# Three column tiles side by side at the head of a recurrent decoder step, with its x loads put in another order

## The chip, the cores and the metric

The kernel runs on one core of a Trainium2 chip. The metric is the device time of one execution in microseconds (us). The kernel before takes 847.57 us, the median of three runs (846.61 to 848.86).

## What is computed

One layer of a hybrid decoder step for a prompt of 256 positions and eight single decode positions, 264 columns in all. A combined projection of x (2048 wide) feeds two branches, an mLSTM and a gated linear attention, whose outputs are gated, projected and normalised:

```python
p = x @ w_in                                   # 2048 -> 12,312 columns
(qk_pre, a_v, a_i, a_f, a_o, a_z, b_q, b_k, b_v, b_g, b_z, g_a, g_b) = _split_cols(p)
conv = causal depthwise conv (width 4) of qk_pre + conv_b
qk = jax.nn.silu(conv)
h, C_new, n_new, m_new = _mlstm(q, k, v, itil, logf, C, n, m)
o, S_new = _gla(gq, gk, gv, loga, S)
merged = jax.nn.sigmoid(g_a) * (ya @ w_pa) + jax.nn.sigmoid(g_b) * (yb @ w_pb)
out = _layernorm(ALPHA * x + merged @ w_out, ln_g, ln_b)
```

## The kernel before

The work is a list of units (line 61), each one tile of 128 output columns: 16 for the convolved q and k, one small one for the gates, then the other projections. A unit has 16 tiles of the contraction, in four chunks of four (`KC`, lines 45 and 46); a chunk of a unit's weights is a piece (line 162), 256 KB. Below, u1c2 is unit 1, chunk 2. x lies in four chunks as well, 528 KB each.

Every fp32 operand is split into a high half (ACT rounds it to fp32r, lines 204 and 211) and a low half (DVE subtracts, lines 206 and 212). `parts` (line 214) then issues three matmuls for each contraction tile: high weights by high x (line 225), high by low (226), low by high (230), 48 for a unit, all into one accumulator of the pool `ps_m`, which has three (line 97). `parts` is a generator: it yields ahead of each chunk, so a caller can interleave units.

Raw weights arrive through `load_raw` (line 167) in tiles of two pieces; there are four such tiles (`RAW_BUFS`). `cast_piece` (line 187) splits the next piece; there are nine buffers for split pieces (`CAST_BUFS`). Its instructions carry a high priority (line 203). The order on PE is that of the source (line 40, `MANUAL`); ACT, DVE and SP get theirs from a planner, by priority and readiness. All loads go through SP's queue.

At the head (lines 1085 to 1099) x is loaded and split chunk by chunk, and units 0 and 1 are worked on side by side: chunk 0 of both, chunk 1 of both, and so on. The first eight pieces are put in that order by line 163. After this the units come one by one (line 1102); units 0 and 1 are only evacuated there. `e_qk` (line 255) evacuates a q or k unit: ACT reads the accumulator (line 261), DVE reads it three times (line 263, the shifted taps), ACT once more (line 266), each of them ahead of the buffer's next use; a sigmoid and a product follow.

Of the kernel before, what the change touches and what calls it, by code (L numbers as in the profile page):

```python
# [23 lines left out]
T = L + NB  # L24
# [20 lines left out]
KC = 4  # L45
NC = KT // KC
KR = 8
RAW_BUFS = 4
CAST_BUFS = 9
LA = CAST_BUFS - NC  # L50
RA = (RAW_BUFS - 1) * KR // KC

COL = {}
# [32 lines left out]
def body(ctx, tc, xT, wbig, wsmall, par, cmask, lmask, sel, rowc, gate, wgu, cT, sT, nst, cst, lnr,  # L86
         y, yd, pC, pn, pm, pconv, pS, sC, sn, sm, sS):
    nc = tc.nc
    V, A, G, PE = nc.vector, nc.scalar, nc.gpsimd, nc.tensor
# [11 lines left out]
    def t4(shape, name, dt=F32):  # L101
        return b4.tile(shape, dt, tag="b4", name=name)
# [21 lines left out]
    def side_ps():  # L124
        return ps_s.tile([128, 512], F32, tag="sd", name="sd")
# [14 lines left out]
    ones = const.tile([128, 128], F32, name="ones")  # L140
# [10 lines left out]
    x_hi = [const.tile([128, 4, T], F32R, name=f"xh{i}") for i in range(4)]  # L151
    x_lo = [const.tile([128, 4, T], F32R, name=f"xl{i}") for i in range(4)]

    def f(ap):
        return ap.bitcast(F32)

    pieces = []
    idx = 0
    for n, (kind, j) in enumerate(UN):
        bi = None if kind == "small" else idx  # L160
        idx += kind != "small"
        pieces += [(n, c, bi) for c in range(NC)]
    pieces[0:2 * NC] = [pieces[u * NC + c] for c in range(NC) for u in range(2)]
    raws, his, los = {}, {}, {}
    nxt = {"dma": 0, "cast": 0}

    def load_raw():
        i = nxt["dma"]
        if i >= len(pieces):
            return  # L170
        r = wraw_p.tile([128, KR, 128], F32, tag="raw", name="raw")
        per = KR // KC
        runs = []
        for q in range(per):
            n, c, bi = pieces[i + q]
            w = 128 if bi is not None else SMALL
            raws[i + q] = r[:, q * KC:q * KC + KC, 0:w]
            if runs and runs[-1][0] == n and runs[-1][2] == c * KC:
                runs[-1][2] += KC
            else:  # L180
                runs.append([n, c * KC, c * KC + KC, q * KC, bi, w])
        for n, k0, k1, o, bi, w in runs:
            src = wbig[bi] if bi is not None else wsmall
            nc.sync.dma_start(out=r[:, o:o + k1 - k0, 0:w], in_=src[:, k0:k1, :])
        nxt["dma"] += per

    def cast_piece():
        i = nxt["cast"]
        while nxt["dma"] <= i:
            load_raw()  # L190
        n, c, bi = pieces[i]
        w = 128 if bi is not None else SMALL
        r = raws.pop(i)
        if bi is None:
            hl = whi_p.tile([128, KC, 128], F32R, tag="hi", name="hl")
            A.copy(out=hl[:, :, 0:w], in_=r)
            V.tensor_tensor(out=hl[:, :, w:2 * w], in0=r, in1=f(hl[:, :, 0:w]), op=ALU.subtract)
            his[n, c], los[n, c] = hl[:, :, 0:2 * w], None
            nxt["cast"] += 1
            return  # L200
        h = whi_p.tile([128, KC, 128], F32R, tag="hi", name="hi")[:, :, 0:w]
        lo = wlo_p.tile([128, KC, 128], F32R, tag="lo", name="lo")[:, :, 0:w]
        with tc.high_priority(offset=PRIO):
            A.copy(out=h, in_=r)  # L204
            E = G if POOL_LO[0] <= n < POOL_LO[1] and c in POOL_C else V
            E.tensor_tensor(out=lo, in0=r, in1=f(h), op=ALU.subtract)  # L206
        his[n, c], los[n, c] = h, lo
        nxt["cast"] += 1

    def split(hi, lo, src):  # L210
        A.copy(out=hi, in_=src)
        V.tensor_tensor(out=lo, in0=src, in1=f(hi), op=ALU.subtract)

    def parts(n, k0, k1, rhs, base=0):

        small = UN[n][0] == "small"
        m = 2 * SMALL if small else 128
        ps = ps_m.tile([128, 512], F32, tag="mm", name="mm")
        out = ps[0:m, 0:T]
        for k in range(k0, k1):  # L220
            if k % KC == 0:
                yield ps[:, 0:T]
            wh = his[n, k // KC][:, k % KC, :]
            rh, rl = rhs(k - base)
            PE.matmul(out, lhsT=wh, rhs=rh, start=(k == k0), stop=False)  # L225
            PE.matmul(out, lhsT=wh, rhs=rl, start=False, stop=small and k == k1 - 1)  # L226
            if small:
                continue
            wl = los[n, k // KC][:, k % KC, :]
            PE.matmul(out, lhsT=wl, rhs=rh, start=False, stop=(k == k1 - 1))  # L230

    def group(*a, **kw):
        for ps in parts(*a, **kw):
            pass
        return ps
# [595 lines left out]
    def e_pab(pa, pb, j):  # L831
        g = gtiles[j // 2]
        i = 2 * (j % 2)
        ga, gb = g[:, i, :], g[:, i + 1, :]
        V.tensor_tensor(out=ga, in0=ga, in1=pa, op=ALU.mult)
        V.tensor_tensor(out=gb, in0=gb, in1=pb, op=ALU.mult)
        V.tensor_tensor(out=ga, in0=ga, in1=gb, op=ALU.add)
        split(mh.t(j), ml.t(j), ga)
# [50 lines left out]
    def ln_shift(j):  # L889

        xt = ln["x", j]
        V.scalar_tensor_tensor(out=xt, in0=xt, scalar=ALPHA, in1=ln["c"], op0=ALU.mult, op1=ALU.subtract)
# [187 lines left out]
    with tc.manual_schedule(engines=MANUAL):  # L1080
        V.memset(ones, 1.0)
        V.memset(inv256, 1.0 / 256.0)
        V.memset(eps_c, EPS)
        V.memset(one_c, 1.0)
        first = [parts(u, 0, 16, x_rhs) for u in range(2)]
        head = {}
        for i in range(4):
            xr = t4([128, 4, T], "xr")
            nc.sync.dma_start(out=xr, in_=xT[:, 4 * i:4 * i + 4, :])
            if 4 * i % KC == 0:  # L1090
                for _ in range(2 * KC // KR):
                    load_raw()
            split(x_hi[i], x_lo[i], xr)
            for u in range(2) if (4 * i + 4) % KC == 0 else ():
                cast_piece()
                head[u] = next(first[u])
        for u in range(2):
            for _ in first[u]:
                pass
        nc.sync.dma_start(out=par_sb, in_=par)  # L1100
        nc.sync.dma_start(out=cst_sb, in_=cst)
        for n, (kind, j) in enumerate(UN):
            st['n'] = n
            while nxt["cast"] < NC * (n + 1) + LA and nxt["cast"] < len(pieces):
                cast_piece()
                while nxt["dma"] < min(nxt["cast"] + RA, len(pieces)):
                    load_raw()
            if kind == "pab":
                pa = group(n, 0, 8, lambda k: (st["yah"].t(k), st["yal"].t(k)))
                pb = group(n, 8, 16, lambda k: (st["ybh"].t(k), st["ybl"].t(k)), base=8)  # L1110
                e_pab(pa, pb, j)
            elif kind == "out":
                ln_pre(j)
                if j >= 8:
                    ln_shift(j)
                ps = group(n, 0, 16, lambda k: (mh.t(k), ml.t(k)))
                e_out(ps, j)
            else:
                ps = head[n] if n in head else group(n, 0, 16, x_rhs)
                if n == 0:  # L1120
                    g_conv_prep()
                if n == 4:
                    V.tensor_copy(out=im_sb, in_=ident)
                    sel_t["sel"] = t4([16, 8, 128], "sel_sb")
                    for dst, src in ((gate_sb, gate), (wgu_sb, wgu), (sel_t["sel"], sel), (rc_sb, rowc), (cm_sb, cmask), (lm_sb, lmask)):
                        nc.sync.dma_start(out=dst, in_=src)
                if kind == "qk":
                    for _ in e_qk(ps, j):
                        pass
                elif kind == "small":  # L1130
                    add(g_gates(ps), True)
                elif kind == "av":
                    e_v(ps, j, "avt", "avd")
                elif kind == "bv":
                    e_v(ps, j, "bvt", "bvd")
                elif kind == "bq":
                    e_plain(ps, j, "gq", Q_SCALE)
                elif kind == "bk":
                    e_plain(ps, j, "gk")
                elif kind in ("ao", "az"):  # L1140
                    e_raw(ps, 2 * j + (kind == "az"), "ozr", 4, g_oz)
                elif kind == "bz":
                    e_raw(ps, j, "bzr", 4, g_bz)
                elif kind in ("ga", "gb"):
                    e_raw(ps, 2 * j + (kind == "gb"), "gr", 4, g_g)
            pump(BUDGET)
            if kind == "gb" and j == 15:
                drain()
        ln_final()
# [141 lines left out]
```

## Time and profile before

| | |
|---|---|
| median of three runs | 847.57 us |
| profiled execution | 848.32 us |
| its span, first to last instruction | 846.5 us |
| mean granted TensorE clock | 0.994 |
| busy: PE, DVE, ACT, POOL | 97%, 74%, 56%, 10% |

All times in the rows are us from the span's start, of one profiled execution. PE is the matmul engine, DVE the vector engine, ACT the scalar engine, SP the engine whose queue issues the loads. In a tile's name `hi` and `lo` are the halves of a weight piece, `xh` and `xl` those of x, `raw` and `xr` the loaded data, `mm` a unit's accumulator, `cacc` the convolution's sum. A timeline merges equal neighbours: "x2" is two instructions, and the second number then covers both.

### The profile page before, as it was taken

The numbers are of one execution on the slowest core, as the hardware profiler recorded it, in microseconds if no ns is written. First come the engines' busy times: TensorE is split into PE (matmuls) and PEld (weight loads), VectorE is DVE, ScalarE is ACT, GpSimd is POOL, SyncE is SP. The second block draws the span as 40 slices with busy tenths as digits, with TensorE's granted clock in tenths as the row PEclk, the third lists the DMA queues.
The fourth block names the chain that finished last, engine by engine and source line by source line (L and its number), as shares of the span: only waits on it lengthen the run. The fifth ranks groups of instructions, "written<-read, shape, count | busy, mean of one in ns | idle before, by whom it ended". The sixth has DMA issues, their size and how long they took to land.

```text
span 846.5 us, 17762 instructions
## 1 busy us (share of the span) xinstructions
PE 824.9 (97%) x6773; PEld 811.4 (96%) x6773; DVE 630.0 (74%) x1354; ACT 470.6 (56%) x896; POOL 82.7 (10%) x103
## 2 busy tenths in 40 slices
PE   6999999999999999999999999988999999999996
PEld 6999999999999999999999999988999999999995
DVE  6987768645586897876786799989895777767862
ACT  5755567545464565655655665353765444455643
POOL 0000000001010210110110202220300000000211
PEclk9999999999999999999999999999999999999998
DMA  8765565545666765676787656776656665576513
GB/s 318 243 213 178 161 188 167 155 149 166 209 211 214 259 198 188 210 232 213 238 284 227 193 164 215 256 244 216 216 170 224 185 182 178 179 260 206 179 51 103
DMA packets 50917, 170.21 MB, mean 201 GB/s; under 512 B 7936, under 2 KB 8880, under 8 KB 50832
## 3 DMA queue, kind: packets, MB, share of 16 engines
q1 hardware_dynamic: 46704, 154.66, 57.8%
q0 software_dynamic: 4128, 14.42, 4.5%
q8 instruction: 53, 0.87, 0.4%
q14 instruction: 32, 0.26, 0.1%
HBM read 152.36 MB, written 16.58 MB: 200 GB/s over the span
## 4 chain that ended last, share of the span: by engine, by line
PE 89%; DMA 4%; DVE 3%; issue 1%; ACT 1%; POOL 0%; SPq 0%; ACTq 0%; POOLq 0%; DVEq 0%
PE mm L225 27%; PE mm L226 27%; PE mm L230 27%; DMA raw<-wbig 1%; DVE lo L206 1%; DMA cch<-cT 1%; PE sd L467 1%; DVE sch L788 1%; DMA sch<-sT 1%; PE sd L423 1%; DMA sS<-sch 1%; PE sd L699 1%; DVE scr L790 1%; DMA ga<-rows 1%; PE sd L403 0%
## 5 line engine op out<-in xcount | busy, mean ns | idle before, releaser
L206 DVE TENSOR_TENSOR lo<-raw,hi 128x512 fp32r<-128x512 f32 x512 | 354.8, 702 | 137.8 <-ACT hi L204 132.9
L204 ACT CAST hi<-raw 128x512 fp32r<-128x512 f32 x512 | 310.2, 618 | 255.8 <-PE mm L226 207.3
L225 PE MATMUL mm<-xh,hi 128*128 128x264 f32 x1536 | 442.4, 288 | 8.1 <-ACT hi L204 7.4
L230 PE MATMUL mm<-xh,lo 128*128 128x264 f32 x1536 | 436.8, 284 | 4.7 <-DVE lo L206 4.7
L226 PE MATMUL mm<-xl,hi 128*128 128x264 f32 x1536 | 436.7, 284 | 0.0
L225 PEld LDWEIGHTS mm<-xh,hi 128*128 128x128 f32 x1536 | 290.7, 189 | 10.2 <-ACT hi L204 7.4
L230 PEld LDWEIGHTS mm<-xh,lo 128*128 128x128 f32 x1536 | 289.4, 188 | 5.7 <-DVE lo L206 5.6
L226 PEld LDWEIGHTS mm<-xl,hi 128*128 128x128 f32 x1536 | 291.0, 189 | 0.2
L225 PE MATMUL mm<-mh,hi 128*128 128x264 f32 x256 | 72.7, 284 | 0.0
L226 PE MATMUL mm<-ml,hi 128*128 128x264 f32 x256 | 72.6, 284 | 0.0
L230 PE MATMUL mm<-mh,lo 128*128 128x264 f32 x256 | 72.3, 283 | 0.0
L226 PEld LDWEIGHTS mm<-ml,hi 128*128 128x128 f32 x256 | 48.2, 188 | 0.0
L225 PEld LDWEIGHTS mm<-mh,hi 128*128 128x128 f32 x256 | 48.1, 188 | 0.0
L230 PEld LDWEIGHTS mm<-mh,lo 128*128 128x128 f32 x256 | 48.1, 188 | 0.0
L564 DVE SCALAR_TENSOR_TENSOR cch<-kb,avd,cch 128x256 f32<-128x256 f32 x64 | 33.1, 551 | 8.0 <-POOL kb L493 4.1
L551 ACT ACTIVATE cch<-cch,decb 128x256 f32<-128x256 f32 x64 | 28.9, 501 | 13.8 <-DMA cch<-cT 13.8
L226 PE MATMUL mm<-ybl,hi 128*128 128x264 f32 x128 | 36.5, 285 | 0.0
L226 PE MATMUL mm<-yal,hi 128*128 128x264 f32 x128 | 36.4, 284 | 0.0
L225 PE MATMUL mm<-yah,hi 128*128 128x264 f32 x128 | 36.4, 284 | 0.0
L230 PE MATMUL mm<-yah,lo 128*128 128x264 f32 x128 | 36.3, 283 | 0.0
L230 PE MATMUL mm<-ybh,lo 128*128 128x264 f32 x128 | 36.2, 283 | 0.0
L225 PE MATMUL mm<-ybh,hi 128*128 128x264 f32 x128 | 36.2, 283 | 0.0
(330 smaller groups left out, 865.5 us busy)
## 6 DMA issues: line engine op xcount, KB each, us to landing
raw<-wbig SPq DMA_DIRECT2D x252, 512.0 KB
cch<-cT SPq DMA_DIRECT2D x16, 512.0 KB
sC<-cch POOLq DMA_DIRECT2D x16, 512.0 KB, 4.7
sch<-sT SPq DMA_DIRECT2D x8, 512.0 KB
sS<-sch POOLq DMA_DIRECT2D x8, 512.0 KB, 6.7
xr<-xT SPq DMA_DIRECT2D x4, 528.0 KB
raw<-wbig SPq DMA_DIRECT2D x8, 256.0 KB
y<-yt SPq DMA_DIRECT2D x8, 256.0 KB
```

Source lines behind the costliest of these rows:

```text
L204: A.copy(out=h, in_=r)
L206: E.tensor_tensor(out=lo, in0=r, in1=f(h), op=ALU.subtract)
L225: PE.matmul(out, lhsT=wh, rhs=rh, start=(k == k0), stop=False)
L226: PE.matmul(out, lhsT=wh, rhs=rl, start=False, stop=small and k == k1 - 1)
L230: PE.matmul(out, lhsT=wl, rhs=rh, start=False, stop=(k == k1 - 1))
L423: PE.matmul(S[:, o:o + n], lhsT=kT.t(2 * h + d)[:, s0:s0 + 128], rhs=qT.t(2 * h + d)[:, t0:t0 + n], start=(d == 0), stop=(d == 1))
L467: PE.matmul(CN[:, 0:VC], lhsT=kw[:, s, d * 128:d * 128 + 128], rhs=vt[h // 2][:, s, h % 2, :], start=(s == 0), stop=(s == 1))
L551: A.activation(out=c[:, b, :], in_=c[:, b, :], func=AF.Copy, scale=decb[:, h, b0 + b:b0 + b + 1])
L564: V.scalar_tensor_tensor(out=c[:, b, :], in0=kb[:, b, :], scalar=avd[:, 2 * h + e, b0 + b:b0 + b + 1], in1=c[:, b, :], op0=ALU.mult, op1=A ...
L699: PE.matmul(pl[s0:s0 + m, 4 * hf + h, n0:n0 + w].rearrange("p (n s) -> p n s", s=hs), lhsT=K[:, h, hf * 128 + s0:hf * 128 + s0 + m], rhs=r ...
L788: V.scalar_tensor_tensor(out=cc, in0=kb[:, b, :], scalar=bvd[:, 2 * h + e, b:b + 1], in1=cc, op0=ALU.mult, op1=ALU.add)
L790: V.scalar_tensor_tensor(out=scr2[:, 0:128], in0=cc, scalar=1.0, in1=qb[:, b, :], op0=ALU.mult, op1=ALU.mult, accum_out=oT.t(2 * h + e)[:, ...
```

## The change

Three units are worked on side by side at the head in place of two (`HU`), so twelve pieces stand in the interleaved order. The raw tile that holds u0c0 and u1c0 and x chunk 0 are loaded as half of x chunk 0, u0c0, the other half, u1c0. The remaining x chunks are queued up front, each followed by one raw tile, ahead of the first raw tile that has to wait for a buffer. x chunk 0 is split in halves, with the first piece's cast between them. Ahead of everything, PE gets nine matmuls of a tile of ones by itself (`WARM`), whose result is not used.

```diff
--- before.py
+++ after.py
@@ -48,6 +48,8 @@
 RAW_BUFS = 4
 CAST_BUFS = 9
 LA = CAST_BUFS - NC
+HU = 3
+WARM = 9
 RA = (RAW_BUFS - 1) * KR // KC
 
 COL = {}
@@ -160,11 +162,11 @@
         bi = None if kind == "small" else idx
         idx += kind != "small"
         pieces += [(n, c, bi) for c in range(NC)]
-    pieces[0:2 * NC] = [pieces[u * NC + c] for c in range(NC) for u in range(2)]
+    pieces[0:HU * NC] = [pieces[u * NC + c] for c in range(NC) for u in range(HU)]
     raws, his, los = {}, {}, {}
     nxt = {"dma": 0, "cast": 0}
 
-    def load_raw():
+    def load_raw(between=None):
         i = nxt["dma"]
         if i >= len(pieces):
             return
@@ -179,7 +181,9 @@
                 runs[-1][2] += KC
             else:
                 runs.append([n, c * KC, c * KC + KC, q * KC, bi, w])
-        for n, k0, k1, o, bi, w in runs:
+        for q, (n, k0, k1, o, bi, w) in enumerate(runs):
+            if q and between:
+                between()
             src = wbig[bi] if bi is not None else wsmall
             nc.sync.dma_start(out=r[:, o:o + k1 - k0, 0:w], in_=src[:, k0:k1, :])
         nxt["dma"] += per
@@ -1082,19 +1086,33 @@
         V.memset(inv256, 1.0 / 256.0)
         V.memset(eps_c, EPS)
         V.memset(one_c, 1.0)
-        first = [parts(u, 0, 16, x_rhs) for u in range(2)]
-        head = {}
+        warm = side_ps()
+        for _ in range(WARM):
+            PE.matmul(warm[:, 0:128], lhsT=ones, rhs=ones, start=True, stop=True)
+        first = [parts(u, 0, 16, x_rhs) for u in range(HU)]
+        head, xr = {}, [t4([128, 4, T], "xr") for _ in range(4)]
+
+        def load_x(i, k=0, n=4):
+            nc.sync.dma_start(out=xr[i][:, k:k + n], in_=xT[:, 4 * i + k:4 * i + k + n, :])
+
+        def split_x(i, k=0, n=4):
+            split(x_hi[i][:, k:k + n], x_lo[i][:, k:k + n], xr[i][:, k:k + n])
+
+        load_x(0, 0, 2)
+        load_raw(lambda: load_x(0, 2, 2))
+        for i in range(1, 4):
+            load_x(i)
+            load_raw()
         for i in range(4):
-            xr = t4([128, 4, T], "xr")
-            nc.sync.dma_start(out=xr, in_=xT[:, 4 * i:4 * i + 4, :])
-            if 4 * i % KC == 0:
-                for _ in range(2 * KC // KR):
-                    load_raw()
-            split(x_hi[i], x_lo[i], xr)
-            for u in range(2) if (4 * i + 4) % KC == 0 else ():
-                cast_piece()
+            for k, n in ((0, 2), (2, 2)) if i == 0 else ((0, 4),):
+                split_x(i, k, n)
+                if k == 0:
+                    cast_piece()
+            for u in range(HU):
+                if u:
+                    cast_piece()
                 head[u] = next(first[u])
-        for u in range(2):
+        for u in range(HU):
             for _ in first[u]:
                 pass
         nc.sync.dma_start(out=par_sb, in_=par)
```

## Rows read from the trace of the kernel before

**Rows 1.** Part 1 of the page: busy us, share of the span, instructions.

```profile
...
PE 824.9 (97%) x6773; PEld 811.4 (96%) x6773; DVE 630.0 (74%) x1354; ACT 470.6 (56%) x896; POOL 82.7 (10%) x103
...
```

**Rows 2.** Part 4 of the page: the chain's share by engine.

```profile
...
PE 89%; DMA 4%; DVE 3%; issue 1%; ACT 1%; POOL 0%; SPq 0%; ACTq 0%; POOLq 0%; DVEq 0%
...
```

**Rows 3.** Waits of PE: total us, times, longest us.

```profile
...
PE mm L225 <- ACT hi L204: 7.4, 1, 7.4
PE mm L230 <- DVE lo L206: 4.7, 3, 2.6
...
```

**Rows 4.** Timeline of PE at the start: start us, length us.

```profile
...
7.39 0.59 PE L225 MATMUL mm<-xh,hi 128*128 128x264 f32 x1 [7.39 <-ACT hi L204]
...
10.71 0.37 PE L226 MATMUL mm<-xl,hi 128*128 128x264 f32 x1
10.92 0.28 PE L230 MATMUL mm<-xh,lo 128*128 128x264 f32 x1
...
```

**Rows 5.** Windows of 1 us; last columns clock, DMA share, GB/s.

```profile
...
5.00:6.00 1.00, 0.00 (x0) 0.00 (x0) 0.46 (x1) 0.51 (x1) 0.00 (x0) 1.00 1.07 251
9.00:10.00 1.00, 1.00 (x6) 1.00 (x6) 0.14 (x1) 1.00 (x2) 0.00 (x0) 1.00 1.05 424
...
```

**Rows 6.** Timeline of SP's DMA issues at the start.

```profile
...
6.72 0.33 SPq L1089 DMA_DIRECT2D xr<-xT  x1
7.40 1.67 SPq L184 DMA_DIRECT2D raw<-wbig  x2
9.43 0.33 SPq L1100 DMA_DIRECT2D par_sb<-par  x1
...
```

**Rows 7.** Timeline of ACT, 0 to 40 us.

```profile
...
4.43 1.07 ACT L211 CAST xh<-xr 128x1056 fp32r<-128x1056 f32 x1 [2.43 <-DMA xr<-xT]
6.72 1.30 ACT L204 CAST hi<-raw 128x512 fp32r<-128x512 f32 x2 [1.22 <-DMA raw<-wbig]
8.75 1.07 ACT L211 CAST xh<-xr 128x1056 fp32r<-128x1056 f32 x1 [0.73 <-DMA xr<-xT]
...
19.59 0.57 ACT L261 ACTIVATE cacc<-mm,par_sb 128x264 f32<-128x264 f32 x1 [0.74 <-PE mm L230]
...
24.07 0.17 ACT L266 COPY co<-mm 128x11 f32<-128x11 f32 x1 [0.29 <-DVE cacc L263]
...
33.66 0.56 ACT L261 ACTIVATE cacc<-mm,par_sb 128x264 f32<-128x264 f32 x1
...
36.41 0.17 ACT L266 COPY co<-mm 128x11 f32<-128x11 f32 x1 [1.16 <-DVE cacc L263]
...
```

**Rows 8.** Timeline of DVE, 0 to 40 us.

```profile
...
0.82 0.17 DVE L1081 MEMSET ones<- 128x128 f32 x1 [0.82 <-PEq L1280]
...
9.86 1.26 DVE L212 TENSOR_TENSOR xl<-xr,xh 128x1056 fp32r<-128x1056 f32 x1 [1.11 <-ACT xh L211]
...
20.30 0.47 DVE L263 SCALAR_TENSOR_TENSOR cacc<-mm,par_sb,cacc 128x255 f32<-128x255 f32 x1
...
20.77 1.28 DVE L206 TENSOR_TENSOR lo<-raw,hi 128x512 fp32r<-128x512 f32 x2
...
22.36 1.28 DVE L206 TENSOR_TENSOR lo<-raw,hi 128x512 fp32r<-128x512 f32 x2
23.57 0.47 DVE L263 SCALAR_TENSOR_TENSOR cacc<-mm,par_sb,cacc 128x253 f32<-128x253 f32 x1
...
```

**Rows 9.** Chain, 193 to 195 us: an fp32 matmul of 128 columns.

```profile
...
194.12 0.22 PE sd L444 x2
...
```

**Rows 10.** Timeline of PE around its longest late wait.

```profile
...
583.30 0.39 PE L230 MATMUL mm<-xh,lo 128*128 128x264 f32 x1 [2.59 <-DVE lo L206]
...
584.40 0.42 PE L226 MATMUL mm<-xl,hi 128*128 128x264 f32 x1
...
587.48 0.41 PE L225 MATMUL mm<-xh,hi 128*128 128x264 f32 x1
...
```

**Rows 11.** Window of 1 us behind that wait.

```profile
...
585.00:586.00 1.00, 1.00 (x7) 1.00 (x6) 1.00 (x6) 0.80 (x2) 0.00 (x0) 0.50 0.87 307
...
```

## The prediction

> **What bounds the kernel now.** I read the page's busy shares first, then the chain, PE's waits, and the first 40 us by engine. The reader is to see a kernel that TensorE sets: PE is busy 97% of the span [rows 1] and makes 89% of the chain [rows 2]. Its waits are few [rows 3]: 7.4 us in one piece before the first matmul, and 4.7 us in three waits for a low half much later. So the change works on the only large idle piece, and what it can win is the moment from which PE runs without a gap, no more.
>
> The head in numbers: the first matmul stands at 7.39, the fourteenth at 10.71, the fifteenth at 10.92 [rows 4]. The first fourteen are 0.22 us apart, the later ones 0.12, and PE never waits again in the head. Each matmul of the slow kind is 0.42 us long, as those in a stretch with a granted clock of 0.50, that is 1.2 GHz, far later [rows 10, 11]; the granted-clock column says 1.00 at the start, so there I go by the durations. Units 0 and 1 take 96 matmuls, unit 2 takes 48, so unit 3's first is the 145th: 10.92 + 130 x 0.12 = 26.5. That is my marker. All of the change is done by then, and behind it PE has no idle piece to give back until the few waits of rows 3.
>
> **The change part by part.**
>
> *Order of loads.* Arrivals can be read off SP and ACT: SP's tenth issue goes at 6.72, the eleventh at 7.40, the thirteenth at 9.43 [rows 6], each just when the DMA eight places ahead (u0c0, u1c0, u0c1; unit 0, chunk 0 and so on) has landed; ACT's casts of x start at 4.43 and 8.75, when x chunks 0 and 1 land [rows 7]. In bytes: 528 KB by 4.43, 784 by 6.72, 1040 by 7.40, 1568 by 8.75, 1824 by 9.43. The queue moved 251 GB/s in 5:6 and 424 in 9:10 [rows 5], with the engines busy in both, so bytes in queue order set the arrivals. The new order is x0a 264 KB, u0c0 (520), x0b (784), u1c0 (1040), x1 (1568), u2c0 (1824), u0c1, x2 and so on. Hence u0c0 at about 4.4 (6.7 if it is the weights' first read that is slow), x0b 6.7, u1c0 7.4, x1 8.75, u2c0 9.4. x3 becomes the eleventh issue and waits for x0b at 6.7; it was the tenth and left at 6.72, so nothing moves. The sixth tile of pieces waits for a raw buffer, behind all x loads, and joins a queue that is still full. Cost: 0.
>
> The lower rate at the start could belong to the start or to the small pieces. If it goes, some 0.17 MB per us (424 less 251) over 2 us is 0.35 MB, at 0.42 MB per us 0.8 us earlier. I take 0.3 and keep 0 to 0.8.
>
> Two halves in place of one x chunk are one issue more on SP, 0.33 us [rows 6]; SP has the time. The Trainium skill's page "DMA: Bandwidth & Descriptors" (Rules for kernel authors) speaks against small transfers and wants at least 1 MiB in each for full bandwidth. The rows show a 256 KB piece landing 0.68 us behind the load ahead of it (6.72 to 7.40, 8.75 to 9.43), and 528 KB taking 1.35 (7.40 to 8.75), the same rate; so the trace does not bear the rule out in a full queue, and I charge nothing.
>
> *PE's early start.* u0c0 at 4.4 plus a cast of 0.65 (two in 1.30 [rows 7]) gives a first matmul at about 5.1, 2.3 us sooner (7.35 by the other end). This doesn't carry through. k = 0 and 1 are six matmuls; k = 2 needs x0b, 6.7 plus half casts of about 0.55 and 0.65 (estimates, half of 1.07 and of 1.26 [rows 7, 8]), so 7.95. u1c0's low half is ready at 8.75, and its 12 matmuls end by 10.2. Unit 2 is now in the same chunk: u2c0 lands at 9.4, ACT has x1 in hand from 8.75 to 9.73, the high half is ready at 10.4; DVE does x1's low half from 9.86 [rows 8] to 11.05 and then the piece's to 11.7 (the other way round, both still end there). PE gets two matmuls of u2c0 before, ten after 11.7, and enters chunk 1 at 12.9. From here each chunk is 36 matmuls, 4.3 us, against DVE's 1.26 + 3 x 0.64 = 3.2 and DMA's 1296 KB, 3.2 us at the late rate: no more waits. 108 x 0.12 = 13.0, so 25.9, and 25.6 with the 0.3. Gain before the marker: 0.9 us (0.6 to 1.4).
>
> *Warm-up.* Nine fp32 matmuls of 128 columns, 0.22 us each at full clock [rows 9], twice that at half, so 2.0 to 4.0 us from about 1.05 (ones is written at 0.82 to 0.99 [rows 8]): over by 5.1, in idle time. They may save the 14 slow matmuls, 14 x 0.10 = 1.4 us. But those would fall before 12.9, where PE waits for data anyway. I take 0; bounds: 0.5 lost, if the clock is still low past 12.9, to nothing gained. By the Trainium skill, "TensorE: Matmul & The Clock Gate" (Part 1: The HAM clock gate), the array stands at its lower clock until activity releases it; by that alone the sum would be 1.4 us better. The trace agrees on the low start, not on its being on the path here.
>
> *What is late next: PSUM.* There are three accumulators for units. With two units in the head, unit 3 takes unit 0's. Unit 0 ended at 19.59 (ACT's line 261 starts [rows 7]); the last read of its accumulator is line 266 at 24.07, ending 24.24: 4.65 us of evacuation, because between its three DVE steps from 20.30 to 23.57 stand two pairs of low halves, at 20.77 and 22.36 [rows 8]. Wanted at 26.5: 2.3 us of slack. With three units interleaved, unit 0 ends only 24 matmuls, 2.9 us, before unit 3 wants the same buffer: at 25.6 - 2.9 + 0.2 = 22.9. Weight tiles still arrive two pieces at a time and their casts carry the higher priority, so the same steps stand between. Bounds: 2.9 us, as unit 2's evacuation from 33.66 to 36.58 [rows 7], and 4.65. I take the middle, 3.8: free at 26.7. PE waits 1.1 us (0.2 to 2.0). What is queued behind that matmul on PE is everything; ACT and DVE fill the cast buffers meanwhile and get their backlog done.
>
> *Sum.* Marker at 26.7 against 26.5: +0.2 us (25.8 to 27.85 with all ends, so -0.7 to +1.35). The profiled execution took 848.32 us (span 846.5), 0.75 over the median; the change of +0.2 on the median 847.57 gives **847.8**.
>
> **Rivals.**
> 1. *The evacuation keeps up.* The scheduler puts unit 0's three steps ahead of the casts and PE never waits: 25.9 to 25.2 against 26.5, -0.6 to -1.3: **846.6**. For it: unit 2's took 2.9 us. Against it: unit 0's took 4.65 under the same stream of tiles.
> 2. *Slower: the wait for unit 0's accumulator, and the clock behind it.* Evacuation 4.65 on the late marker: 27.85, +1.35, with PE idle near 2 us. After a wait of 2.59 at 583.30 the matmuls from 584.40 to 587.48, 15 of them, ran 0.22 apart [rows 10], at a granted clock of 0.50 [rows 11]: 1.5 us lost. Together +2.85: **850.4**. It decides from an idle piece of about 2 us on; under that I expect only the wait.
> 3. *The order of ACT, DVE and SP shifts further on.* Nothing behind 40 us is changed in the source, but their instructions are put in order by a planner, and a shift of three units' work could take away or double the late waits: 4.7 us [rows 3] and 1.5 of slow clock. Half of it is 3.1: **844.5**, or **850.7** the other way.
> 4. *The halves do nothing*, if the first matmuls wait for the whole of x chunk 0: first matmul near 7.9 and not 5.1, but the path runs over u2c0 at 9.4 all the same: **847.8**, as forecast.
>
> **How the numbers follow.** Forecast (with rival 4) 0.42; rival 1 0.25; rival 2 0.13; rival 3 0.12 faster, 0.08 slower. What this kernel's measurement can tell from no change is about 0.3%, 2.5 us: under 845.0 or over 850.1. Faster takes rival 3's share and a corner of rival 1 and of the forecast (other terms too small): 0.20; slower most of rival 2 and of rival 3's other side: 0.17; same 0.63. The range 845.0 to 850.6 takes in both ends of the sum and leaves about 0.2 out; the forecast's own is 846.9 to 848.9.
>
> **What would show it.** Right: a matmul at 5 to 6 us, gaps until 12 or 13, then none until a wait of the 145th head matmul (line 225 of unit 3) for line 266 or 263, of about 1 us; that matmul at 26 to 28. Slow matmuls only before 13 would bear out the warm-up's zero. Wrong: u2c0 landing before 8.5 or PE gapless from 8 on (then the gain is larger); no wait at unit 3 (rival 1); matmuls 0.22 apart behind it (rival 2); PE's waits behind 300 us unlike those of rows 3 (rival 3).

## The result, and the profile after

The changed kernel takes 854.31 us (median of four runs, 853.55 to 856.83), the kernel before, timed beside it, 848.22. The ratio is 1.0087 with an interval of 1.0069 to 1.0104: 6.1 us slower by the medians, 7.4 by the ratio, outside the predicted range. Its profiled execution, the slowest of the four, took 856.83 us with a span of 855.0, 8.5 more than the span before. The profiled execution of run e5 further down fell into a slower state (1358.90 us at a mean granted clock of 0.559), so nothing is read from its trace.

PE's waits in the changed kernel, total us, times, longest us; the lines stand beside [rows 3]:

```profile
...
PE mm L234 <- DVE lo L210: 4.9, 3, 3.6
PE sd L703 <- DVE gq L710: 2.3, 2, 1.9
PE mm L229 <- ACT xh L215: 2.1, 1, 2.1
PE mm L229 <- ACT co L270: 1.8, 1, 1.8
...
PE mm L229 <- ACT hi L208: 0.7, 1, 0.7
...
```

The long wait at the start is gone: 0.7 us of line 229 (225 before) is left for the first weights, and 1.0 for the tile of ones that the warm-up reads. In its place stand 2.1 us for a half of x and 1.8 us for line 270 (266 before), the last reader of an accumulator. The timeline of PE's head (start us, length us) answers to [rows 4]:

```profile
...
1.04 4.21 PE L1091 MATMUL sd<-ones 128*128 128x128 f32 x18 [1.04 <-DVE ones L1085]
5.99 0.39 PE L229 MATMUL mm<-xh,hi 128*128 128x264 f32 x1 [0.73 <-ACT hi L208]
...
6.71 0.39 PE L234 MATMUL mm<-xh,lo 128*128 128x264 f32 x1 [0.22 <-DVE lo L210]
...
7.18 0.28 PE L234 MATMUL mm<-xh,lo 128*128 128x264 f32 x1
9.58 0.59 PE L229 MATMUL mm<-xh,hi 128*128 128x264 f32 x1 [2.12 <-ACT xh L215]
10.39 0.59 PE L230 MATMUL mm<-xl,hi 128*128 128x264 f32 x1 [0.22 <-DVE xl L216]
...
16.06 0.36 PE L234 MATMUL mm<-xh,lo 128*128 128x264 f32 x1
16.25 0.28 PE L229 MATMUL mm<-xh,hi 128*128 128x264 f32 x1
...
```

```profile
...
29.61 0.28 PE L234 MATMUL mm<-xh,lo 128*128 128x264 f32 x1
31.64 0.39 PE L229 MATMUL mm<-xh,hi 128*128 128x264 f32 x1 [1.76 <-ACT co L270]
...
```

The warm-up ends at 5.25 (each of its nine matmuls is recorded as two); the first real matmul stands at 5.99 and not at 7.39, and the six of the first half of chunk 0 have the short lengths, 0.28 and 0.39, with one wait of 0.22 among them and the last three 0.12 us apart. Then PE idles to 9.58. The matmuls behind the gap are 0.59 and then 0.42 long, 27 of them, the last at 16.06. Unit 3's first matmul, my marker, stands at 31.64. Before the change it is the 145th recorded:

```profile
...
26.66 0.28 PE L225 MATMUL mm<-xh,hi 128*128 128x264 f32 x1
...
```

In the windows (the last three columns are granted clock, DMA share and GB/s; compare [rows 5] and [rows 11]) the clock falls at 9.4, after 1.9 us without a matmul, to 0.50, its lower level (1.2 GHz), and comes back at 16.2:

```profile
...
5.00:6.00 1.00, 0.27 (x3) 0.02 (x1) 0.03 (x1) 0.62 (x1) 0.00 (x0) 1.00 0.84 216
8.00:9.00 1.00, 0.00 (x0) 0.00 (x0) 0.00 (x0) 0.62 (x2) 0.00 (x0) 1.00 1.02 402
9.00:10.00 1.00, 0.42 (x1) 0.29 (x1) 0.97 (x2) 0.76 (x2) 0.00 (x0) 0.69 1.05 420
...
15.00:16.00 1.00, 1.00 (x6) 1.00 (x6) 0.96 (x2) 0.89 (x1) 0.00 (x0) 0.50 1.07 379
16.00:17.00 1.00, 1.00 (x10) 1.00 (x9) 0.78 (x1) 1.00 (x3) 0.00 (x0) 0.90 1.02 380
...
```

What ended the gap can be read on ACT, beside [rows 7]:

```profile
...
3.52 0.63 ACT L215 CAST xh<-xr 128x528 fp32r<-128x528 f32 x1 [1.51 <-DMA xr<-xT]
5.32 0.62 ACT L208 CAST hi<-raw 128x512 fp32r<-128x512 f32 x1 [1.17 <-DMA raw<-wbig]
8.38 0.62 ACT L208 CAST hi<-raw 128x512 fp32r<-128x512 f32 x1 [2.44 <-DMA raw<-wbig]
8.90 0.63 ACT L215 CAST xh<-xr 128x528 fp32r<-128x528 f32 x1
9.77 1.07 ACT L215 CAST xh<-xr 128x1056 fp32r<-128x1056 f32 x1 [0.24 <-DMA xr<-xT]
...
27.00 0.57 ACT L265 ACTIVATE cacc<-mm,par_sb 128x264 f32<-128x264 f32 x1 [4.41 <-PE mm L234]
...
31.42 0.17 ACT L270 COPY co<-mm 128x11 f32<-128x11 f32 x1 [0.74 <-DVE cacc L267]
...
```

The first half of x lands at 3.5, u0c0 at 5.3, u1c0 at 8.4 and x chunk 1 at 9.8. The second half of chunk 0 is split only at 8.90, behind the cast of u1c0, though that half had landed by 7.55: SP's eleventh issue, which by the pattern of [rows 6] waits for it, left then.

```profile
...
7.55 0.33 SPq L1096 DMA_DIRECT2D xr<-xT  x1
...
```

Unit 0's evacuation runs from 27.00 to 31.59, 4.6 us, and on DVE (beside [rows 8]) two pairs of low halves stand between its three steps once more:

```profile
...
27.61 0.48 DVE L267 SCALAR_TENSOR_TENSOR cacc<-mm,par_sb,cacc 128x255 f32<-128x255 f32 x1 [3.72 <-ACT cacc L265]
...
28.11 1.29 DVE L210 TENSOR_TENSOR lo<-raw,hi 128x512 fp32r<-128x512 f32 x2
...
29.71 1.28 DVE L210 TENSOR_TENSOR lo<-raw,hi 128x512 fp32r<-128x512 f32 x2
30.91 0.47 DVE L267 SCALAR_TENSOR_TENSOR cacc<-mm,par_sb,cacc 128x253 f32<-128x253 f32 x1
...
```

The 4.98 us at the marker can be split. From the eighth matmul at 10.39 to the 145th are 137 steps, 16.4 us at 0.12; it is as if PE had begun at 9.55 and not 7.39, +2.2. The slow steps cost 2.9 us on top, against 2.0 before, +0.9 (2.7 and 1.85 by the slow steps alone; the rest is that 0.12 is rounded down). The accumulator wait adds 1.9 between two matmuls. The other 3.5 us of the longer span come later. There the profile has 1.0 more of waits and one spell of half clock between 312 and 359 us, and a spell behind the long wait near 590 that is twice as long as before; what each of them costs is not shown. Both profiled executions were above the medians of their kernels, this one by 2.5 us and the one before by 0.75.

### The profile page after: what moved, and what is told of

It reads as the page before. It is cut to its first block, busy times and chain, and to the rows that moved or that the text cites. A ratio compares the mean times of both kernels' runs of the same rounds, so it can differ in the third digit from the quotient of the medians.

```text
span 855.0 us, 17803 instructions
## 1 busy us (share of the span) xinstructions
PE 833.7 (98%) x6791; PEld 819.1 (96%) x6791; DVE 631.9 (74%) x1355; ACT 471.0 (55%) x897; POOL 81.0 (9%) x103
```

## The experiments

Each run was timed beside the kernel before on the same chip, in three groups (e1 to e4, e5 to e8, e9 to e12), so between groups it is the ratios that compare. The marker is read from one profiled execution.

| run | edit | marker | ratio to before (interval) |
|---|---|---|---|
| changed kernel | | 31.64 | 1.0087 (1.0069 to 1.0104) |
| e1 | changed, two units | 29.73 | 1.0056 (1.0034 to 1.0077) |
| e2 | changed, no warm-up | 30.77 | 1.0067 (1.0043 to 1.0090) |
| e3 | changed, fourth accumulator | 29.86 | 1.0030 (1.0017 to 1.0044) |
| e4 | changed, second half of x split first | 29.84 | 1.0049 (1.0029 to 1.0069) |
| e5 | e3 and e4 together | not read | 1.0019 (1.0010 to 1.0029) |
| e6 | changed, x chunk 0 whole | 31.85 | 1.0064 (1.0044 to 1.0083) |
| e7 | before, nine warm-up matmuls | 27.02 | 1.0022 (1.0010 to 1.0034) |
| e8 | before, fourteen | 27.23 | 1.0036 (1.0021 to 1.0051) |
| e9 | halves and order of loads alone | 29.75 | 1.0043 (1.0029 to 1.0057) |
| e10 | three units, x loads queued up front, alone | 30.70 | 1.0048 (1.0035 to 1.0061) |
| e11 | e10, fourth accumulator | 27.07 | 1.0000 (0.9990 to 1.0010) |
| e12 | e6, fourth accumulator | 27.29 | 1.0006 (0.9994 to 1.0019) |

The theory was that three things add up: the wait for unit 0's accumulator, the gap behind the halves of x, and the clock that falls behind the gap. The rivals were the third unit by itself, the warm-up, and the planner's order far behind the head.

**e1**

```diff
-HU = 3
+HU = 2
```

> The changed kernel with two units side by side in place of three; loads, halves and the warm-up stay. The marker is the first matmul of unit 3, 26.6 us before the change and 31.6 after it. Theory: three costs add up there, an accumulator wait of 1.8 that only three units cause, a gap of 2.1 at 7.5 to 9.6 because the second half of x chunk 0 is cast behind piece u1c0 on ACT, and a slow clock to 16.2 that follows the gap. So only the accumulator wait goes: marker 29 to 30, time 2 us under the changed kernel's 854.3, about 852. Rival (three units are the whole cost): marker 26 to 27, time 847 to 848.

Marker 29.73, ratio 1.0056. The theory's marker, and the rival is out: with two units the gap (7.64 to 9.46 between matmuls) and the slow clock stay, and the marker is still 3.1 us late. The time is 1.8 us higher than the marker says.

**e2**

```diff
-WARM = 9
+WARM = 0
-        warm = side_ps()
```

> The changed kernel without the nine matmuls of ones. Theory: the gap and the accumulator wait stay; the first matmul stands at 6.0 as with them, but at half clock, and the clock rises once PE has been busy for some us behind the gap, as at 10.9 before the change; marker 30 to 32, time within 1.5 us of 854.3. Rival A (the warm-up's early rise is what makes the clock fall again and stay low to 16.2): slow matmuls end by 14, marker 29.5 to 30.5, time 852.5. Rival B (the warm-up helps): marker over 32, time 856.

Marker 30.77, ratio 1.0067. The interval overlaps the changed kernel's, so what the warm-up costs or gives there is not resolved. In its trace the matmuls are slow to 14.3, as rival A had it, and not to 16.2; but in e9, also without a warm-up and with the same gap, they are slow to 15.8, so one execution doesn't decide this. Here a slow spell stands behind the accumulator wait, from 31.2 to 34.6.

**e3**

```diff
-        ps = ps_m.tile([128, 512], F32, tag="mm", name="mm")
+        ps = side_ps() if n == 3 else ps_m.tile([128, 512], F32, tag="mm", name="mm")
```

> The changed kernel with unit 3's accumulator taken from the other pool, which is idle then, so that unit 3 need not wait for unit 0's evacuation. Theory: the wait of 1.8 (2.0 between matmuls) at 29.6 goes, all else ahead of it stays; marker 29.6, time 2 us less, about 852.3. Rival (the lost time is made up in a later wait, or the order of ACT and DVE behind 300 us is what costs): marker 29.6, but time 854 as after the change.

Marker 29.86, near what was expected, and 850.35 us: 4 less than the changed kernel and not 2. The wait for line 270 is gone from PE's list. The late part of this profile is shorter too (the shift against before falls from 3.2 at the marker to 1.7 at the end of the span), so the time has more in it than the wait.

**e4**

```diff
-                split_x(i, k, n)
+                with tc.high_priority(offset=PRIO if k else 0):
+                    split_x(i, k, n)
```

> The changed kernel with the split of the second half of x chunk 0 put ahead of the cast of u1c0 on ACT and DVE. Theory: the gap at 7.5 to 9.6 shrinks to about 1 us, since that half has landed by 7.55 (SP's eleventh issue) and takes 0.63 and 0.70 to split; the clock then does not fall or is low for less long; marker 28 to 30, time 1.5 to 3.5 us less, 851 to 853. Rival (the data of three units come too late in any order): the gap only moves to u1c0, which lands at 8.4, the clock falls all the same, marker 31 to 31.6, time 854.

Marker 29.84, 852.11 us, as the theory had it. ACT, in the order that the edit gives:

```profile
...
4.92 0.62 ACT L208 CAST hi<-raw 128x512 fp32r<-128x512 f32 x1 [0.81 <-DMA raw<-wbig]
6.60 0.63 ACT L215 CAST xh<-xr 128x528 fp32r<-128x528 f32 x1 [1.06 <-DMA xr<-xT]
8.57 0.62 ACT L208 CAST hi<-raw 128x512 fp32r<-128x512 f32 x1 [1.34 <-DMA raw<-wbig]
...
```

The half of x lands by 6.60 and is split ahead of u1c0. The clock doesn't fall in the head. But PE now waits seven times up to 14 us, and the last of these shows that the pieces come late:

```profile
...
13.04 0.39 PE L234 MATMUL mm<-xh,lo 128*128 128x264 f32 x1 [0.87 <-DVE lo L210]
...
```

That is the 27th matmul, u2c0's third. From there to 27.92 PE is done with 144; then comes the accumulator wait of 1.8, to 29.84. With the gap and the clock mended the head still has 1.3 us more than before ahead of that wait.

**e5**: both edits above.

> The changed kernel with both repairs: the second half of x chunk 0 split ahead of u1c0, and unit 3's accumulator from the other pool. Theory: the wait of 2.0 between matmuls at 27.8 goes, so the marker (unit 3's first matmul, 26.66 before the change, 31.64 after, 29.84 with the first repair alone) stands at 27.8 to 28.0, and the time is 1.2 us over the kernel before, 848 to 850, since pieces of three units land later than they are wanted. Rival (the three repairs overlap and the planner's later order costs the rest): marker under 27, time 851 or more.

849.08 us, ratio 1.0019, inside what was expected. What is left over the kernel before is 1.6 us. By elimination it is put down to the loads in halves and the warm-up, since e11 below has three units and a fourth accumulator at no cost; no run takes them apart.

**e6**

```diff
-        load_x(0, 0, 2)
-        load_raw(lambda: load_x(0, 2, 2))
-        for i in range(1, 4):
+        for i in range(4):
             load_x(i)
             load_raw()
...
-            for k, n in ((0, 2), (2, 2)) if i == 0 else ((0, 4),):
+            for k, n in ((0, 4),):
```

> The changed kernel with x chunk 0 loaded and split whole, as before the change; three units, the warm-up and the order of the other loads stay. Theory A (halves of 264 KB make the first loads slower): u1c0 lands at 7.4 as before the change, against 8.4 with the halves; the first matmul stands at 7.4 and not 6.0, the gap at 7.5 to 9.6 is gone, the clock is at full rate or falls once; marker 29 to 30 with an accumulator wait of about 2. Rival (the arrivals are slow because x chunk 1 and the weights are queued close behind): u1c0 lands at 8.4 here too and the marker stays over 30.5.

Half a miss. u1c0 lands at 7.74, the gap is gone, and PE is done with the 144 matmuls by 27.2, 2.5 us sooner than in the changed kernel. Yet the marker is 31.85: the wait for line 270 has grown to 4.5 us. ACT shows why:

```profile
...
24.90 1.14 ACT L208 CAST hi<-raw 128x512 fp32r<-128x512 f32 x2 [0.28 <-DVE lo L210]
25.95 0.56 ACT L265 ACTIVATE cacc<-mm,par_sb 128x264 f32<-128x264 f32 x1
...
31.11 0.62 ACT L208 CAST hi<-raw 128x512 fp32r<-128x512 f32 x1 [2.16 <-DMA raw<-wbig]
31.64 0.16 ACT L270 COPY co<-mm 128x11 f32<-128x11 f32 x1
...
```

In this kernel's order two more casts stand ahead of unit 0's first read, which begins at 25.95 though unit 0's last matmul began at 24.2, and one more, which waits 2.16 us for its weights, just ahead of the last read. A cast that waits for a DMA holds the accumulator.

**e7, e8**: the same warm-up put into the kernel before.

```diff
+        warm = side_ps()
+        for _ in range(9):
+            PE.matmul(warm[:, 0:128], lhsT=ones, rhs=ones, start=True, stop=True)
         first = [parts(u, 0, 16, x_rhs) for u in range(2)]
```

e8 has 14 in place of 9.

> The kernel before with nine matmuls of ones ahead of its first real one, and nothing else of the change. They end at about 5.2, the first real matmul stands at 7.4. Theory (an idle piece between the warm-up and the work gives the clock back): the clock's state at 7.4 changes from run to run, so between 0 and 14 slow matmuls are saved; marker 25.2 to 28, time within 1.5 us of the kernel before. Rival (a warm-up pays whatever follows): marker 25.2, time 1.4 us less.

> The kernel before with fourteen matmuls of ones, which end at 6.5 to 7.6, next to the first real matmul at 7.4. Theory (it is the gap behind the warm-up that matters): no slow matmul in the head, marker 25.2, time 1.4 us less than before, 846.4. Rival (the end of the head isn't on the path, the late waits take it back): marker 25.2, time as before, 847.8.

Both were missed, e7 narrowly: its marker, 27.02, is in the range, its time 1.6 us over the kernel before where 1.5 was the bound. Neither saves anything; they are slower by 0.22% and 0.36%. With nine, the clock is up at 7.64 and down again from 8.0 to 11.4, with 12 slow matmuls against 14 before. With fourteen there is no slow spell in the head, but u1c0 and x chunk 1 land at 8.37 and 9.80 in that execution (7.40 and 8.75 before), PE waits three times between 11.0 and 12.8, and the marker is 27.23. In both a wait also shows up that the kernel before just avoids, for unit 1's accumulator at unit 4 (there line 266 ends at 32.25 and unit 4 begins at 32.46). Before, then in e7 and in e8:

```profile
...
32.08 0.17 ACT L266 COPY co<-mm 128x11 f32<-128x11 f32 x1 [0.41 <-DVE cacc L263]
...
```

```profile
...
33.73 0.39 PE L225 MATMUL mm<-xh,hi 128*128 128x264 f32 x1 [0.76 <-ACT co L266]
...
```

```profile
...
34.46 0.39 PE L225 MATMUL mm<-xh,hi 128*128 128x264 f32 x1 [1.27 <-ACT co L266]
...
```

**e9, e10**: one part of the change at a time on the kernel before. As edits to the changed kernel, e9 is those of e1 and e2 together, e10 those of e2 and e6.

> The kernel before with the new loads alone: two units, no warm-up, x chunk 0 in halves with u0c0 between them, the other x loads queued up front. Theory (the halves make the first loads land later and leave a gap on PE that the cast order widens): u1c0 lands at 8.3 to 8.8 against 7.4, a gap of about 2 us after the sixth matmul, marker (first matmul of unit 3, 26.66 before) 28 to 29.5, time 2 to 3 us over the kernel before, near 850. Rival (the halves cost nothing without the warm-up and the third unit): marker 26 to 27, time 847.

> The kernel before with three units side by side alone: x chunk 0 whole, no warm-up. Theory (unit 0's accumulator is wanted 2.9 us after its last matmul, and its evacuation takes 4.6 us or more): PE waits 1.8 to 4.5 us for line 270 at unit 3, marker 28.5 to 32, time 3 to 5 us over the kernel before, 850 to 852. Rival (what costs is the gap and the clock behind the halves): no wait of over 0.5, marker 26 to 27, time 847.

e10 came out as the theory had it, 851.22 us (0.48%). e9, 850.51 us (0.43%), is a little over its ranges, with the marker at 29.75 and 3.1 us by the medians. Its u1c0 lands at 7.94, a little under the range given, and PE idles from 7.65 to 9.14 for the second half of x:

```profile
...
7.23 0.42 PE L234 MATMUL mm<-xh,lo 128*128 128x264 f32 x1
9.14 0.59 PE L229 MATMUL mm<-xh,hi 128*128 128x264 f32 x1 [1.49 <-ACT xh L215]
...
36.78 0.39 PE L229 MATMUL mm<-xh,hi 128*128 128x264 f32 x1 [1.06 <-ACT co L270]
...
```

The last line is the wait for unit 1's accumulator at unit 4 again, behind the marker, so e9's time is not the arrivals and the gap alone (e1 has 0.43 us of it). In e10 the first matmul is at 6.98; with no gap and no warm-up 26 matmuls are slow there, to 13.15, where the kernel before had 14. PE is done with 144 at 27.5, and then waits 3.1 us for the accumulator; behind it the clock falls, which it did not do in the changed kernel:

```profile
...
12.71 0.42 PE L229 MATMUL mm<-xh,hi 128*128 128x264 f32 x1
...
27.34 0.28 PE L234 MATMUL mm<-xh,lo 128*128 128x264 f32 x1
30.70 0.59 PE L229 MATMUL mm<-xh,hi 128*128 128x264 f32 x1 [3.08 <-ACT co L270]
31.09 0.42 PE L230 MATMUL mm<-xl,hi 128*128 128x264 f32 x1
...
```

```profile
...
29.00:30.00 1.00, 0.00 (x0) 0.00 (x0) 1.00 (x3) 0.62 (x1) 0.00 (x0) 1.00 0.71 147
31.00:32.00 1.00, 1.00 (x6) 1.00 (x6) 0.13 (x2) 0.80 (x1) 0.00 (x0) 0.50 0.61 197
34.00:35.00 1.00, 1.00 (x10) 1.00 (x9) 1.00 (x3) 0.15 (x1) 0.00 (x0) 1.00 0.33 127
...
```

**e11, e12**: e10 and e6, each with e3's edit.

> Three units alone as in the run beside it, with unit 3's accumulator from the other pool. Theory: the wait at unit 3 goes, the marker stands at 26.5 to 27.5, and the time is within 1 us of the kernel before, 847 to 848. Rival (three units cost something beside the accumulator, by the order that ACT and DVE get): time over 849.5.

> The changed kernel with x chunk 0 whole and unit 3's accumulator from the other pool; the nine matmuls of ones stay. Theory: without gap and accumulator wait only the warm-up is left beside the run without it; ahead of unit 0 PE still idles from about 5 to 7.4, and what the warm-up saves of slow matmuls PE loses to weights that land later than it wants them; marker 26 to 27.5, time 847 to 849. Rival (the warm-up pays once the two waits are gone): marker 25.3, time 846 or less.

e11 is the kernel before to within 0.1%: marker 27.07, ratio 1.0000. All that three units cost alone goes with the accumulator. PE's waits in it:

```profile
...
PE mm L229 <- ACT hi L208: 7.5, 1, 7.5
PE mm L234 <- DVE lo L210: 3.3, 3, 2.4
PE mm L229 <- ACT gr L589: 0.7, 1, 0.7
PE sd L703 <- DVE gq L710: 0.4, 1, 0.4
```

There is no line for 270 any more. e12 differs from it by the warm-up alone and is not faster (1.0006, interval across 1): the rival that a warm-up pays once the waits are gone falls. e12 also closes the account: it keeps the third unit, the order of the other loads and the warm-up, and drops only the halves of x chunk 0 and the wait for the accumulator. Without these two the whole 0.87% is gone, to within e12's interval.

## Why the prediction was wrong

The reading of what bounds the kernel held in the main: what PE loses in the head is not made up behind it. Going through the steps:

*Order of loads, halves at no charge.* This step failed. u0c0 at 4.4, the second half at 6.7, u1c0 at 7.4 and x chunk 1 at 8.75 were forecast; 5.3, up to 7.55, 8.4 and 9.8 were measured. Executions differ here: with the same loads e4 had the second half by 6.60. Across the runs x chunk 1 lands at 9.79 on average in the six kernels with halves (9.34 to 10.21, e5 left out) and at 9.17 in the seven with a whole chunk 0 (8.75 to 9.80, the kernel before among them). I took the spacing of a full queue, 0.68 us for 256 KB, for the first microseconds too, where the rows showed 251 GB/s. The guess that the low rate might go away was the wrong way round. The halves with their order cost 0.43% alone (e9), 3.6 us. The Trainium skill's advice for large loads ("DMA: Bandwidth & Descriptors", Rules for kernel authors), which I set aside by a row from a full queue, goes the way that the runs went, by 0.6 us of mean arrival; no run here separates the size of the loads from their number.

*The early start doesn't carry through.* Right in kind: the first matmul came at 5.99 (5.1 forecast) and won nothing. But I had the second half of x split ahead of u1c0 and the next matmul at 7.95. ACT and DVE have their order from the planner, casts carry the higher priority, and the half went behind u1c0: 9.58. That this happened is seen on ACT after the change; e4 turns it round and takes 1.8 us off the marker.

*The warm-up at no charge, since slow matmuls fall before 12.9.* Failed. The clock was up for six matmuls, fell after PE had idled from 7.5 on, and stayed low to 16.2: 27 slow matmuls against 14. The Trainium skill's rule that activity releases the clock ("TensorE: Matmul & The Clock Gate", Part 1) is borne out by the six fast matmuls; what it bought was gone after the gap. In the terms of the sum: 12.9 was forecast for the 37th matmul, the first of chunk 1, which is 8.6 for the first and 8.3 with the 0.3 taken off; 9.55 was measured, 1.2 us later, and the 2.9 us of slow steps behind it were forecast as 0. (The 14 slow matmuls before cost 1.85 and not 1.4, since the first four stand further apart.) Not all of the 2.9 could have been won: in e4, where the clock stays up, PE waits for pieces, the 27th matmul stands at 13.04 where 11.7 was forecast, and the accumulator wait begins only 1.8 us sooner than in the changed kernel. Alone, on the kernel before, the warm-up costs 0.22% (e7); in e12 nothing that can be told.

*The accumulator.* Right in its place and its reason, too small in size. Evacuation was put at 3.8 between 2.9 and 4.65 and came out at 4.6; PE lost 1.9 us against 1.1 (0.2 to 2.0), 0.8 more. I took the middle of two rows where the nearer row, unit 0's own, was right. And the upper bound was no bound: by itself, with PE faster ahead of it, the wait is 3.1 us (e10) or 4.5 (e6), since the static order of ACT and DVE puts casts that wait for weights between the reads (0.95 us of such waiting in e10, 2.16 in e6). Removing it is worth 0.48% (e10 to e11).

*The sum.* Marker +0.2 forecast (-0.7 to +1.35), +4.98 measured: +2.2 start, +0.9 clock, +1.9 accumulator. Against the forecast of 26.7 the marker is 4.9 us late: 1.2 by the start, 2.9 by slow steps put at nothing, 0.8 by the accumulator. Rival 2 had the accumulator wait with the clock falling behind it; that pair stands in e2, e6 and e10, not in the changed kernel, whose clock fell earlier. Its 2.85 us would have been too little as well, and its condition, an idle piece of about 2 us, does not tell the cases apart: behind a wait of 1.76 us the clock fell in e2 and stayed up in the changed kernel. Rival 4 was not the case: the first six matmuls did not wait for the second half.

*Behind the head.* The profile has 3.5 us more there, rival 3's place. The head's shift and the longer time of the two profiled executions differ by -2.3 to +3.5 us across these kernels. The three with a fourth accumulator have -1.6 to -2.3 and the others -0.6 to +3.5, so that edit may win something there too; why is not shown. Half-clock spells of 3.4 or 6.8 us behind the late waits are part of the difference. Whether the changed kernel loses there on average is open: by ratio it is 7.4 us slower, and 5.0 of them are seen at the marker. Why the first loads are slower in halves is open too. In e7 the trace has 1.1 us of the loss, 0.4 at the marker and 0.76 at unit 4; that its profiled span equals that of before says little, since the profiled execution of before was 1.4 us above the median of the runs beside e7.

## What to carry to other kernels

Before more work is put side by side at the start, ask when each accumulator is wanted again and read the time of its whole evacuation, with whatever the planner sets between its reads, from the same place in the trace; the nearest row is better than a mean. A load cut in two for an earlier start is worth nothing if the engine that prepares it takes something else first, and here it was not free in the queue. A warm-up paid in none of these runs: behind a gap the clock was soon down again (changed kernel, e7), and where it stayed up (e8) the loads landed late.

## What the runs showed of the hardware

Six fast matmuls behind a warm-up did not keep the clock up through the gap that followed: it fell 1.9 us into the gap in the changed kernel, 0.6 in e1 and 1.8 in e3, and was up again at 16.2, 15.4 and 16.0. Without the warm-up, behind the same gap, the matmuls were slow to 14.3 (e2) and 15.8 (e9). With neither gap nor warm-up the slow stretch was 3.5 us long in the kernel before (7.39 to 10.9) and 6.2 in e10 (6.98 to 13.15). From 1 to 8 us the DMA engines moved less when the first loads were in halves: 1.43 to 1.62 MB in the six traces with halves (e5 left out), 1.66 to 1.78 in the seven with a whole chunk 0. At 5:6 it was 216 GB/s with a busy share of 0.84 in the changed kernel, against 251 with 1.07 before. And 14 matmuls on a tile that needs no load went with loads that landed up to 1.0 us later in the one profile there is of it (e8), which I can't explain.
